# SSD decay factors of one decoder trunk kernel: repeated rows read back from DRAM in place of matmul broadcasts

## Chip, cores and metric

One Trainium2 chip, one core. The metric is the device time of one launch in microseconds (us). The kernel before took 2094.0 us, the median of three runs (2093.61 to 2096.1).

## The reference, cut to what matters

A decoder trunk with 512 tokens, width 1024 and two layers. Each layer is a half SwiGLU feed-forward, a mixer and a second half feed-forward; the mixer of the first layer is a Mamba-2 SSD (state space) mixer, that of the second an S5 mixer. All values are float32. The change touches the SSD mixer alone. It has 32 heads of 64 channels in 8 groups of 4 heads; the group shares B and C (128 states). Per head, with `cs` the running sum of `dt * A` inside a chunk, the reference computes

```python
seg = cs[:, :, None] - cs[:, None]
decay = exp(where(causal, seg, -inf))
cb = einsum('btgn,bsgn->btsg', cc, bc)
dtx = dt[..., None] * xc
y_diag = einsum('btsgk,bsgkp->btgkp', cb[..., None] * decay, dtx)
y_off = einsum('btgn,bgkpn->btgkp', cc, state) * exp(cs)[..., None]
```

and then carries `state` to the next chunk. The kernel uses four chunks of 128 tokens.

## The kernel before

The work runs as stages: feed-forward, SSD, feed-forward, feed-forward, S5, feed-forward. Tokens lie along the free dimension (512 of them), channels along the 128 partitions. A projection (`proj`, L219) multiplies a 1024-wide block with 24 matmuls of 512 columns: every float32 operand is held as a high and a low part, and three products are made for each of 8 blocks. Its weights come on SyncE's queue (SP) in 512 KB loads with four buffers (`wst`); ScalarE casts the high part (L214), VectorE subtracts for the low part (L216), each with three buffers.

**SSD stage (L273 to L545).** First `dt` is projected, and a chain on VectorE and ScalarE (L285 to L314) makes `dt`, the running sums `cs` (L312) and their exponentials; the heads stand in the partitions, 32 heads four times over. Then come 8 groups (loop at L517). Each makes six projections: two convolutions for B and C, two for the channels x (`conv`, L353, `silu`, L368), and two gates (`gate`, L390). The scan of a group is cut in pieces that lie between the projections of the next group, by the list `pend`, from which `pop` (L376) takes one after each projection:

- `head` (L403): products C·B per chunk into `cb`, transposes of x and B, `dtx`, `wx`, and the previous group's `final`
- after the B projection: `states` (L433) and `decay(0)` (L452)
- after the C projection: `outp(0)` (L468) and `decay(1)`
- after the first x projection: `outp(1)`; after the second: nothing; after the first gate: `norm`.

A head pair is one `e` (two heads). `decay(e)` builds, for each of its two heads, a 128x512 tile whose every row is that head's `cs`, by a matmul with a selecting weight (L458, `cshl` holds `cs` as a high and a low part), and adds the causal mask by a second matmul (L459). ScalarE then takes the exponential out of PSUM with the bias -cs of the row's token (L463, one instruction per chunk), and VectorE multiplies by `cb` (L464). `outp(e)` makes exp(cs) for the pair's 128 channels the same way (L473, L475, L477), multiplies it by C·state (L481, L482), makes the diagonal part (L488: 8 float32 matmuls, each recorded as two instructions) and sums, gates and squares (L491 to L495).

After group 4 the first 8 of 16 row blocks of the output projection are done (`out_rows(0, 8)`), after group 7 the rows 8 to 12, between whose eight column blocks the last group's pieces lie, and then the rows 12 to 16.

**What sets the order.** In the SSD stage TensorE's instructions stand in the order in which the program writes them. The instructions of the other engines and queues are ordered by a scheduler with a timing model of its own, unless `tc.keep_in_program_order` puts one behind the instruction that the program wrote before it on the same engine. Every engine and every queue then works strictly in its order. A PSUM tile is 128x512; there are four tagged "mm" (projections) and four tagged "aux". Tiles of a name rotate over their buffers (two where nothing is given).

Of the kernel before, what the change touches and what calls it, by code (L numbers as in the profile page):

```python
# [9 lines left out]
F32 = mybir.dt.float32  # L10
F32R = mybir.dt.float32r
# [19 lines left out]
def trunk_kernel(ctx, tc, x, ffn1_norm, ffn1_w_in, ffn1_w_out, mix_norm, ffn2_norm, ffn2_w_in, ffn2_w_out,  # L31
# [29 lines left out]
    identr = const.tile([128, 128], F32R, name="identr")  # L61
# [6 lines left out]
    def masks():  # L68

        V.tensor_copy(identr, ident)  # L70
# [202 lines left out]
    def ssd(pr, nxt):  # L273
        w_in, w_out = ssd_in_proj[0], ssd_out_proj[0]
        with ExitStack() as es:
            sc = es.enter_context(tc.tile_pool(name="ssdc", bufs=1))
            sp = es.enter_context(tc.tile_pool(name="ssd", bufs=2))

            wd = wpool.tile([128, KD, 128], F32, name="wst", bufs=4)
# [8 lines left out]
            ax = sp.tile([128, T], F32, name="m")  # L288
            V.scalar_tensor_tensor(ax, v, -1.0, v, op0=OP.mult, op1=OP.max)
            ex = sp.tile([128, T], F32, name="m")  # L290
# [5 lines left out]
            rw = sp.tile([128, T], F32, name="m")  # L296
# [3 lines left out]
            dt = sp.tile([128, T], F32, name="m")  # L300
# [15 lines left out]
            for c in range(4):  # L316
# [4 lines left out]
            pack = sp.tile([128, T], F32, name="m")  # L321
# [4 lines left out]
            cshl = sc.tile([128, T], F32R, name="cshl")  # L326
            S.copy(cshl, cs)
            V.tensor_tensor(cshl[32:64], cs[32:64], cshl[32:64].bitcast(F32), op=OP.subtract)
            sel = sc.tile([128, 32], F32R, name="sel")
            V.memset(sel.bitcast(F32), 0.0)  # L330
            V.tensor_copy(sel[0:32], ident[0:32, 0:32])
            V.tensor_copy(sel[32:64], ident[32:64, 32:64])
            mneg = sc.tile([128, 128], F32R, name="mneg")
            mf = sp.tile([128, 128], F32, name="mf", bufs=1)
            G.memset(mf, 0.0)
            G.affine_select(out=mf, in_=mf, compare_op=OP.is_ge, fill=-1e30, base=0, pattern=[[1, 128]],
                            channel_multiplier=-1)
            V.tensor_copy(mneg, mf)
# [14 lines left out]
            def conv(ct):  # L353
# [4 lines left out]
                raw = sp.tile([128, T + 4], F32, name="raw")  # L358
                G.memset(raw[:, 0:4], 0.0)
# [12 lines left out]

            YH, YL = [None] * 16, [None] * 16
# [25 lines left out]
            def scan(g, BT, CT, XS, SZ):  # L399

                st = {}

                def head():  # L403

                    pcb = aux_ps()
                    for c in range(4):
                        s = slice(c * 128, (c + 1) * 128)
                        PE.matmul(pcb[:, s], BT[:, s], CT[:, s], start=True, stop=True)  # L408
# [17 lines left out]
                    for c in range(3):  # L426
                        s = slice(c * 128, (c + 1) * 128)
                        PE.transpose(pbt[:, s], BT[:, s], ident)
# [809 lines left out]
```

## Time and profile before

| | |
|---|---|
| median of three runs | 2094.0 us |
| the profiled execution, its own time | 2095.47 us |
| its span, first to last instruction | 2093.7 us |
| TensorE busy | 2053.9 us, 98% |
| VectorE busy | 1254.8 us, 60% |
| ScalarE busy | 795.8 us, 38% |
| GpSimd busy | 41.0 us, 2% |
| granted TensorE clock, mean | 0.99 of full speed |
| SSD stage, from the `dt` projection to the last output block | about 383 to 830 us of the span |

PE is TensorE's matmuls, PEld its weight loads, DVE VectorE, ACT ScalarE, POOL GpSimd, SP SyncE's queue. A busy time counts from an instruction's start to its recorded end; matmuls overlap, so the step from one start to the next says what one costs. In the rows further down, "aux" and "mm" are the PSUM tiles, "mm" as an operation's output too. "[0.58 <-ACT ecs L477]" behind a row means that the engine stood idle for 0.58 us before it and that the ScalarE instruction of L477 ended that.

### The profile page before, as it was taken

The numbers are of one execution on the slowest core, as the hardware profiler recorded it, in microseconds if no ns is written. First come the engines' busy times: TensorE is split into PE (matmuls) and PEld (weight loads), VectorE is DVE, ScalarE is ACT, GpSimd is POOL, SyncE is SP. The second block draws the span as 40 slices with busy tenths as digits, with TensorE's granted clock in tenths as the row PEclk, the third lists the DMA queues.
The fourth block names the chain that finished last, engine by engine and source line by source line (L and its number), as shares of the span: only waits on it lengthen the run. The fifth ranks groups of instructions, "written<-read, shape, count | busy, mean of one in ns | idle before, by whom it ended". The sixth has DMA issues, their size and how long they took to land.

```text
span 2093.7 us, 27153 instructions
## 1 busy us (share of the span) xinstructions
PE 2053.9 (98%) x10771; PEld 1691.4 (81%) x10771; DVE 1254.8 (60%) x2156; ACT 795.8 (38%) x1149; POOL 41.0 (2%) x114
## 2 busy tenths in 40 slices
PE   8999999999999999999999999999996999999997
PEld 7888888888888887887788888888886888888886
DVE  6889445778875787557764544343458545444444
ACT  5323233566753664333432332222354333222233
POOL 1000000000000000000000000000011000000000
PEclk9999999999999999999999999999997999999999
DMA  6354643322223213535553363333367133333331
GB/s 180 95 159 159 151 108 84 101 71 71 77 70 89 79 41 113 155 110 162 137 146 98 94 200 91 101 94 99 96 189 236 61 91 101 101 91 88 110 87 58
DMA packets 407631, 232.68 MB, mean 111 GB/s; under 512 B 44168, under 2 KB 395568, under 8 KB 407248
## 3 DMA queue, kind: packets, MB, share of 16 engines
q1 hardware_dynamic: 381920, 203.12, 34.2%
q10 hardware_dynamic: 21440, 13.91, 2.3%
q0 software_dynamic: 4144, 13.92, 2.1%
q8 instruction: 84, 1.38, 0.3%
q14 instruction: 43, 0.35, 0.1%
HBM read 206.21 MB, written 24.18 MB: 110 GB/s over the span
## 4 chain that ended last, share of the span: by engine, by line
PE 94%; DVE 3%; ACT 1%; issue 1%; DMA 0%; DVEq 0%; ACTq 0%
PE mm L223 29%; PE mm L225 29%; PE mm L224 29%; PE aux L488 1%; PE aux L481 0%; PE aux L438 0%; DVE z L969 0%; PE aux L149 0%; PE aux L458 0%; PE aux L225 0%; PE aux L223 0%; PE aux L224 0%; PE aux L408 0%; PE aux L827 0%; PE aux L417 0%
## 5 line engine op out<-in xcount | busy, mean ns | idle before, releaser
L214 ACT CAST whi<-wst 128x1024 fp32r<-128x1024 f32 (+2 forms) x357 | 360.9, 1012 | 935.8 <-PE mm L224 652.0
L223 PE MATMUL mm<-hH,whi 128*128 128x512 f32 x1800 | 705.3, 392 | 2.6 <-ACT whi L214 1.6
L225 PE MATMUL mm<-hH,wlo 128*128 128x512 f32 x1800 | 702.0, 390 | 0.5 <-DVE wlo L216 0.5
L224 PE MATMUL mm<-hL,whi 128*128 128x512 f32 x1800 | 702.2, 390 | 0.0
L216 DVE TENSOR_TENSOR wlo<-wst,whi 128x1024 fp32r<-128x1024 f32 (+2 forms) x357 | 418.9, 1174 | 89.8 <-ACT whi L214 85.5
L223 PEld LDWEIGHTS mm<-hH,whi 128*128 128x128 f32 x1800 | 338.2, 188 | 74.1 <-ACT whi L214 2.0
L225 PEld LDWEIGHTS mm<-hH,wlo 128*128 128x128 f32 x1800 | 338.2, 188 | 72.1 <-DVE wlo L216 1.0
L224 PEld LDWEIGHTS mm<-hL,whi 128*128 128x128 f32 x1800 | 338.3, 188 | 69.4 <-issue 0.6
L224 PE MATMUL mm<-al,whi 128*128 128x512 f32 x704 | 275.5, 392 | 0.0
L225 PE MATMUL mm<-ah,wlo 128*128 128x512 f32 x704 | 275.3, 392 | 0.0
L223 PE MATMUL mm<-ah,whi 128*128 128x512 f32 x704 | 274.6, 392 | 0.0
L252 DVE TENSOR_TENSOR up<-mm,rbc 128x512 f32<-128x512 f32 x88 | 60.7, 690 | 220.0 <-PE mm L225 219.8
L264 DVE SCALAR_TENSOR_TENSOR xT<-mm,xT 128x512 f32<-128x512 f32 x96 | 66.1, 690 | 193.3 <-PE mm L225 193.3
L224 PEld LDWEIGHTS mm<-al,whi 128*128 128x128 f32 x704 | 132.1, 188 | 29.0 <-issue 0.6
L223 PEld LDWEIGHTS mm<-ah,whi 128*128 128x128 f32 x704 | 132.1, 188 | 28.7 <-issue 0.6
L225 PEld LDWEIGHTS mm<-ah,wlo 128*128 128x128 f32 x704 | 132.1, 188 | 28.6 <-issue 0.2
L249 DVE TENSOR_TENSOR gt<-mm,rbc 128x512 f32<-128x512 f32 x88 | 60.7, 689 | 147.9 <-PE mm L225 142.9
L255 ACT CAST ah<-up 128x512 fp32r<-128x512 f32 x88 | 54.9, 624 | 67.8 <-DVE up L253 67.7
L364 DVE SCALAR_TENSOR_TENSOR cv<-raw,cols,cv 128x512 f32<-128x512 f32 x96 | 70.9, 745 | 0.7
L253 DVE TENSOR_TENSOR up<-up,gt 128x512 f32<-128x512 f32 x88 | 60.6, 690 | 7.0 <-ACT whi L214 0.5
L257 DVE TENSOR_TENSOR al<-up,ah 128x512 fp32r<-128x512 f32 x88 | 60.0, 684 | 2.4 <-ACT ah L255 1.4
L250 ACT ACTIVATE gt<-gt 128x512 f32<-128x512 f32 x88 | 55.1, 627 | 11.1 <-DVE gt L249 5.3
(341 smaller groups left out, 1727.4 us busy)
## 6 DMA issues: line engine op xcount, KB each, us to landing
wst<-in_ffn_w_in_dram SPq DMA_DIRECT2D x176, 512.0 KB, 3.9
wst<-in_ffn_w_out_dram SPq DMA_DIRECT2D x64, 448.0 KB, 3.7
wst<-in_ssd_in_proj_dram SPq DMA_DIRECT2D x48, 512.0 KB, 4.0
wst<-in_ffn_w_out_dram SPq DMA_DIRECT2D x32, 512.0 KB, 4.0
opP<-d_P SPq DMA_DIRECT2D x16, 512.0 KB, 5.0
wst<-in_s_glu_w_dram POOLq DMA_DIRECT2D x12, 512.0 KB, 5.0
d_t<-p_cs POOLq DMA_DIRECT2D x8, 512.0 KB, 4.3
wst<-in_ssd_out_proj_dram SPq DMA_DIRECT2D x8, 512.0 KB, 4.2
```

The costliest lines, as they stand in the source:

```text
L214: S.copy(hi, st)
L216: V.tensor_tensor(lo, st, hi.bitcast(F32), op=OP.subtract)
L223: PE.matmul(ps, hi[:, k], H[k], start=first and k == 0, stop=False)
L224: PE.matmul(ps, hi[:, k], L[k], start=False, stop=False)
L225: PE.matmul(ps, lo[:, k], H[k], start=False, stop=last and k == n - 1)
L249: V.tensor_tensor(gt, pg, pr.rbc, op=OP.mult)
L250: S.activation(gt, gt, AF.Silu)
L252: V.tensor_tensor(up, pu, pr.rbc, op=OP.mult)
L253: V.tensor_tensor(up, up, gt, op=OP.mult)
L257: V.tensor_tensor(al, up, ah.bitcast(F32), op=OP.subtract)
L264: V.scalar_tensor_tensor(xT[d], po, 0.5, xT[d], op0=OP.mult, op1=OP.add)
L364: V.scalar_tensor_tensor(cv, raw[:, 1 + j:T + 1 + j], col("cw", j * 32 + ct), cv, op0=OP.mult, op1=OP.add)
```

## The change

The cumulative sums `cs` of the 32 heads are written once to a DRAM tile `d_cs` (32 rows of 512, on SP's queue). `rows(e)` reads them back, on GpSimd's queue: one DMA fills a 128x2x512 tile `dec` whose every partition holds the rows of both heads of the pair (512 KB written into SBUF), and two DMAs of 64 partitions each fill the last 384 columns of `ecs` (96 KB each). GpSimd then masks the `dec` tile in place by one `affine_select` of 1024 elements per partition. `exps(e)` is the same eight exponentials, now in place in SBUF, and one for `ecs`, each put behind what the program wrote before it on ScalarE. `decay(e)` is what is left: one product of 1024 elements per partition by `cb`, put behind what the program wrote before it on VectorE. The matmuls of L458, L459 and L475, their operands (`sel`, `selp`, `cshl`, `mneg`, `identr`) and their making go away.

The places: `rows(0)` stands ahead of `head`, `rows(1)` and `exps(0)` behind `head` and the previous `final`, `exps(1)` between `states` and `decay(0)`. The products C·B and the transposes of B leave `head` and stand between the two gates, behind the previous group's `norm` (`chunk_products`). For the last group an empty piece is put in behind `states`, so that the rest comes one output block later. The convolutions' `raw` tiles become two fixed tiles, whose first four columns are cleared once by VectorE rather than 32 times by GpSimd. The `dt` chain's scratch tiles take the new `dec` shape.

The core of the diff (left out: `identr` and its copy, and context lines):

```diff
             sc = es.enter_context(tc.tile_pool(name="ssdc", bufs=1))
             sp = es.enter_context(tc.tile_pool(name="ssd", bufs=2))
 
+            def dec2():
+                m = sp.tile([128, 2, T], F32, name="dec")
+                return m[:, 0], m[:, 1]
+
+
             wd = wpool.tile([128, KD, 128], F32, name="wst", bufs=4)
...
-            ax = sp.tile([128, T], F32, name="m")
+            ax, ex = dec2()
             V.scalar_tensor_tensor(ax, v, -1.0, v, op0=OP.mult, op1=OP.max)
-            ex = sp.tile([128, T], F32, name="m")
             S.activation(ex, ax, AF.Exp, scale=-1.0)
...
-            rw = sp.tile([128, T], F32, name="m")
+            rw, dt = dec2()
             S.activation(rw, ln, AF.Exp, scale=-1.0)
             V.scalar_tensor_tensor(w1, w1, -1.0, ex, op0=OP.add, op1=OP.subtract)
             V.tensor_tensor(w1, w1, rw, op=OP.mult)
-            dt = sp.tile([128, T], F32, name="m")
             V.scalar_tensor_tensor(dt, v, 0.0, ln, op0=OP.max, op1=OP.add)
             V.tensor_tensor(dt, dt, w1, op=OP.subtract)
...
-            pack = sp.tile([128, T], F32, name="m")
+            pack = dec2()[0]
             V.tensor_copy(pack[0:32], dt[0:32])
             V.tensor_scalar(pack[32:64], cs[32:64], -1.0, None, op0=OP.mult)
             V.tensor_tensor(pack[64:128], dt[64:128], ew[64:128], op=OP.mult)
             tok = sc.tile([128, 4, 128], F32, name="tok")
-            cshl = sc.tile([128, T], F32R, name="cshl")
-            S.copy(cshl, cs)
-            V.tensor_tensor(cshl[32:64], cs[32:64], cshl[32:64].bitcast(F32), op=OP.subtract)
-            sel = sc.tile([128, 32], F32R, name="sel")
-            V.memset(sel.bitcast(F32), 0.0)
-            V.tensor_copy(sel[0:32], ident[0:32, 0:32])
-            V.tensor_copy(sel[32:64], ident[32:64, 32:64])
-            mneg = sc.tile([128, 128], F32R, name="mneg")
-            mf = sp.tile([128, 128], F32, name="mf", bufs=1)
-            G.memset(mf, 0.0)
-            G.affine_select(out=mf, in_=mf, compare_op=OP.is_ge, fill=-1e30, base=0, pattern=[[1, 128]],
-                            channel_multiplier=-1)
-            V.tensor_copy(mneg, mf)
+
+            d_cs = dram.tile([32, T], F32, name="d_cs")
+            nc.sync.dma_start(d_cs, cs[0:32])
+
+            def cs_rows(dst, h, parts):
+                n = dst.shape[-1]
+                G.dma_start(dst, bass.AP(tensor=d_cs.tensor, offset=d_cs.offset + h * T + T - n,
+                                         ap=[[0, parts]] + [[T, k] for k in dst.shape[1:-1]] + [[1, n]]))
+
...
-                raw = sp.tile([128, T + 4], F32, name="raw")
-                G.memset(raw[:, 0:4], 0.0)
+                raws.append(raws.pop(0))
+                raw = raws[0]
...
+            raws = [sc.tile([128, T + 4], F32, name=f"raw{i}") for i in range(2)]
+            for raw in raws:
+                V.memset(raw[:, 0:4], 0.0)
             YH, YL = [None] * 16, [None] * 16
...
-            def scan(g, BT, CT, XS, SZ):
+            def chunk_products(BT, CT):
 
                 st = {}
+                pcb = aux_ps()
+                for c in range(4):
+                    s = slice(c * 128, (c + 1) * 128)
+                    PE.matmul(pcb[:, s], BT[:, s], CT[:, s], start=True, stop=True)
+                st["cb"] = sp.tile([128, T], F32, name="cb", bufs=1)
+                S.copy(st["cb"], pcb)
+                pbt = aux_ps()
+                for c in range(3):
+                    s = slice(c * 128, (c + 1) * 128)
+                    PE.transpose(pbt[:, s], BT[:, s], ident)
+                st["bt"] = sp.tile([128, 384], F32, name="btok", bufs=1)
+                S.copy(st["bt"], pbt[:, :384])
+                return st
+
+            def scan(g, st, CT, XS, SZ):
+
 
                 def head():
 
-                    pcb = aux_ps()
-                    for c in range(4):
-                        s = slice(c * 128, (c + 1) * 128)
-                        PE.matmul(pcb[:, s], BT[:, s], CT[:, s], start=True, stop=True)
-                    st["cb"] = sp.tile([128, T], F32, name="cb", bufs=1)
-                    S.copy(st["cb"], pcb)
                     dtx = sp.tile([128, 4, 256], F32, name="dtx", bufs=1)
...
-                    pbt = aux_ps()
-                    for c in range(3):
-                        s = slice(c * 128, (c + 1) * 128)
-                        PE.transpose(pbt[:, s], BT[:, s], ident)
-                    btok = sp.tile([128, 384], F32, name="btok", bufs=1)
-                    S.copy(btok, pbt[:, :384])
-                    st["dtx"], st["wx"], st["bt"] = dtx, wx, btok
+                    st["dtx"], st["wx"] = dtx, wx
...
-                def decay(e):
-
-                    M = []
+                def rows(e):
+
+                    h = 4 * g + 2 * e
+                    m = sp.tile([128, 2, T], F32, name="dec")
+                    cs_rows(m, h, 128)
+                    ecs = sp.tile([128, T], F32, name="ecs")
+                    for hh in range(2):
+                        cs_rows(ecs[hh * 64:hh * 64 + 64, 128:], h + hh, 64)
+                    G.affine_select(out=m.rearrange("p h (c t) -> p (h c) t", c=4),
+                                    in_=m.rearrange("p h (c t) -> p (h c) t", c=4), compare_op=OP.is_ge, fill=-1e30,
+                                    base=0, pattern=[[0, 8], [1, 128]], channel_multiplier=-1)
+                    st["M", e], st["ecs", e] = m, ecs
+
+                def exps(e):
+                    m = st["M", e]
                     for hh in range(2):
                         h = 4 * g + 2 * e + hh
-                        pE = aux_ps()
-                        PE.matmul(pE, sel[:, h:h + 1].to_broadcast([128, 128]), cshl, start=True, stop=False)
-                        PE.matmul(pE, identr, mneg[:, None, :].to_broadcast([128, 4, 128]), start=False, stop=True)
-                        m = sp.tile([128, T], F32, name="m")
                         for c in range(4):
                             s = slice(c * 128, (c + 1) * 128)
-                            S.activation(m[:, s], pE[:, s], AF.Exp, bias=tok[:, c, 32 + h:33 + h])
-                        V.tensor_tensor(m, m, st["cb"], op=OP.mult)
-                        M.append(m)
-                    st["M", e] = M
+                            tc.keep_in_program_order(
+                                S.activation(m[:, hh, s], m[:, hh, s], AF.Exp, bias=tok[:, c, 32 + h:33 + h]))
+                    ecs = st["ecs", e]
+                    tc.keep_in_program_order(S.activation(ecs[:, 128:], ecs[:, 128:], AF.Exp))
+
+                def decay(e):
+
+                    m = st["M", e]
+                    tc.keep_in_program_order(
+                        V.tensor_tensor(m, m, st["cb"][:, None, :].to_broadcast([128, 2, T]), op=OP.mult))
 
                 def outp(e):
                     M = st["M", e]
 
-                    selp = sp.tile([128, 2, 64], F32R, name="selp")
-                    h0 = 4 * g + 2 * e
-                    V.tensor_copy(selp, sel[:, h0:h0 + 2].bitcast(F32)[:, :, None].to_broadcast([128, 2, 64]))
-                    pe_ = mm_ps()
-                    PE.matmul(pe_, selp.rearrange("p a b -> p (a b)"), cshl, start=True, stop=True)
-                    ecs = sp.tile([128, T], F32, name="ecs")
-                    S.activation(ecs[:, 128:], pe_[:, 128:], AF.Exp)
+                    ecs = st["ecs", e]
                     po = aux_ps()
                     for c in range(1, 4):
                         s = slice(c * 128, (c + 1) * 128)
@@ -485,7 +497,7 @@
                         for hh in range(2):
                             s = slice(c * 128, (c + 1) * 128)
                             k0 = (2 * e + hh) * 64
-                            PE.matmul(py[hh * 64:(hh + 1) * 64, s], st["dtx"][:, c, k0:k0 + 64], M[hh][:, s], start=True,
+                            PE.matmul(py[hh * 64:(hh + 1) * 64, s], st["dtx"][:, c, k0:k0 + 64], M[:, hh, s], start=True,
                                       stop=True)
...
-                return both(head, *fin), [both(states, lambda: decay(0)), both(lambda: outp(0), lambda: decay(1)),
+                rows(0)
+                return both(head, *fin, lambda: rows(1), lambda: exps(0)), [
+                    both(states, lambda: exps(1), lambda: decay(0)), both(lambda: outp(0), lambda: decay(1)),
                                           lambda: outp(1), lambda: None, norm], final
...
@@ -527,9 +541,10 @@
                     SZ.append(gate(2 * g + e, f"sz{e}"))
                     if e == 0:
                         pop()
+                        st = chunk_products(BT, CT)
                 while pend:
                     pop()
-                head, pend, last = scan(g, BT, CT, XS, SZ)
+                head, pend, last = scan(g, st, CT, XS, SZ)
                 if g:
                     head()
                 else:
@@ -537,6 +552,7 @@
                 fin = [last]
                 if g == 4:
                     out_rows(0, 8)
+            pend[1:1] = [lambda: None]
```

## Rows read from the trace of the kernel before

**Rows 1.** The page, parts 1 and 4: busy times, chain that ended last

```profile
PE 2053.9 (98%) x10771; PEld 1691.4 (81%) x10771; DVE 1254.8 (60%) x2156; ACT 795.8 (38%) x1149; POOL 41.0 (2%) x114
...
PE 94%; DVE 3%; ACT 1%; issue 1%; DMA 0%; DVEq 0%; ACTq 0%
```

**Rows 2.** Stretches: length, then busy us of PE, PEld, DVE, ACT, POOL

```profile
511.00:555.00 44.00, 44.00 (x294) 36.58 (x293) 35.38 (x66) 28.84 (x46) 0.41 (x4) 1.00 0.27 73
527.49:536.01 8.52, 8.52 (x52) 7.04 (x51) 7.52 (x12) 6.27 (x15) 0.10 (x1) 1.00 0.23 63
774.00:830.00 56.00, 54.53 (x336) 44.11 (x335) 45.42 (x83) 29.07 (x56) 0.00 (x0) 1.00 0.29 85
```

**Rows 3.** Waits of TensorE's matmuls, 372 to 830 us: total, times, longest

```profile
PE aux L149 <- ACT sq L495: 1.0, 1, 1.0
PE aux L158 <- DVE nw_y L140: 0.9, 1, 0.9
PE aux L481 <- DVE st L448: 0.5, 1, 0.5
```

**Rows 4.** Groups of instructions by line: count, busy us, mean ns, idle before

```profile
L458 PE MATMUL aux<-cshl,sel 128*128 128x512 f32 x32 | 15.0, 468 | 0.0
L475 PE MATMUL mm<-cshl,selp 128*128 128x512 f32 x16 | 6.3, 393 | 0.0
L464 DVE TENSOR_TENSOR m<-m,cb 128x512 f32<-128x512 f32 x32 | 22.0, 688 | 2.4 <-ACT m L463 2.2
```

**Rows 5.** Timeline of TensorE around one `decay(0)`: start us, us

```profile
520.70 0.58 PE L458 MATMUL aux<-cshl,sel 128*128 128x512 f32 x1
521.12 0.40 PE L459 MATMUL aux<-mneg,identr 128*128 128x512 f32 x1
...
521.82 0.39 PE L223 MATMUL mm<-hH,whi 128*128 128x512 f32 x1
```

**Rows 6.** TensorE's timeline around `outp(0)`, `decay(1)` and the next `outp(1)`

```profile
527.29 0.39 PE L475 MATMUL mm<-cshl,selp 128*128 128x512 f32 x1
528.28 1.09 PE L488 MATMUL aux<-m,dtx 128*64 128x128 f32 x16
529.31 0.51 PE L458 MATMUL aux<-cshl,sel 128*128 128x512 f32 x1
...
530.34 0.39 PE L223 MATMUL mm<-hH,whi 128*128 128x512 f32 x1
...
536.80 1.09 PE L488 MATMUL aux<-m,dtx 128*64 128x128 f32 x16
```

**Rows 7.** Timeline of VectorE in the same stretch

```profile
530.30 0.55 DVE L482 TENSOR_TENSOR ecs<-ecs,aux 128x384 f32<-128x384 f32 x1 [0.58 <-ACT ecs L477]
...
538.78 1.23 DVE L216 TENSOR_TENSOR wlo<-wst,whi 128x1024 fp32r<-128x1024 f32 x1 [1.95 <-ACT whi L214]
```

**Rows 8.** GpSimd's mask (ns min/median/max), and a GpSimd copy beside VectorE (timeline)

```profile
L336 POOL TENSOR_SCALAR_AFFINE_SELECT mf<-mf x1: 287/287/287, 383.5 to 383.5; 128x128 f32<-128x128 f32 x1
...
359.86 2.56 POOL L282 COPY wst<-wst 128x256 f32<-128x256 f32 x3 [140.56 <-DVE xT L264]
...
361.28 0.88 DVE L176 TENSOR_TENSOR acc<-acc,sq 128x512 f32<-128x512 f32 x1
...
365.99 0.68 DVE L176 TENSOR_TENSOR acc<-acc,sq 128x512 f32<-128x512 f32 x1
```

**Rows 9.** The page, part 6: 512 KB loads on SP's and GpSimd's queues

```profile
wst<-in_ssd_in_proj_dram SPq DMA_DIRECT2D x48, 512.0 KB, 4.0
wst<-in_s_glu_w_dram POOLq DMA_DIRECT2D x12, 512.0 KB, 5.0
```

**Rows 10.** VectorE's `selp` and `cs` (first and last start); first B projection

```profile
L473 DVE CAST selp<-sel x16: 164/217/218, 384.3 to 755.9; 128x128 fp32r<-128x128 f32 x16
...
L312 DVE TENSOR_TENSOR_SCAN y<-rst,y x1: 1205/1205/1205, 406.7 to 406.7; 128x512 f32<-128x512 f32 x1
...
389.32 0.39 PE L223 MATMUL mm<-hH,whi 128*128 128x512 f32 x1
```

More of the change, by code (lines that the diff above doesn't have):

```diff
@@ L60, in trunk_kernel @@
     make_identity(nc, ident)
-    identr = const.tile([128, 128], F32R, name="identr")
     ones = const.tile([128, 128], F32, name="ones")
@@ L68, in masks @@
     def masks():
-        V.tensor_copy(identr, ident)
         V.tensor_reduce(kmask, ident.rearrange("p (k q) -> p k q", q=8), axis=AX.X, op=OP.add)
```

## Prediction, made before the changed kernel was run

> **What bounds the kernel now.** I read the page first: TensorE is busy for 98% of the span, and 94% of the chain that ended last is TensorE's [rows 1]. That is an average over six stages, so I then read the SSD stage by stretches and by TensorE's waits. In a steady group TensorE is busy for all of the stretch, VectorE for 35 of 44 us, ScalarE for 29, GpSimd for 0.4 [rows 2]. In the whole stage its matmuls wait three times, 2.4 us together: 1.0 us in the first group's scan, 0.9 and 0.5 us in the last's [rows 3]. So here a matmul that goes away is worth its step from start to start, not its recorded 393 or 468 ns [rows 4], as long as nothing that was hidden behind TensorE comes out.
>
> **What goes from TensorE.** 16 head pairs (8 groups, two each) lose four broadcast and mask matmuls in `decay` and one in `outp`. In a first `decay` the step from the first L458 to the next projection is 521.82 - 520.70 = 1.12 us [rows 5], in a second 530.34 - 529.31 = 1.03 us [rows 6]. The first L458 takes a step of 0.42 us, the three behind it 521.82 - 521.12 = 0.70, so 0.233 each [rows 5]: the first stands behind float32 matmuls. I expect that extra to pass to the projection matmul that follows in its place, so four plain steps remain, 4 x 0.233 = 0.93 us; if it vanished, 1.12 and 1.03 would. L475 is a plain step too: it stands behind a projection and is counted 16 times [rows 4]. That is 16 x (0.93 + 0.23) = 18.6 us, at most 16 x 0.23 + 8 x (1.12 + 1.03) = 20.9 us. All of it lies on the path that sets the end.
>
> `chunk_products` moves 7 matmul calls, which cost TensorE the same where they go. They stand right behind the previous group's `norm`, also float32, so as a rule no change between kinds of matmul is added. In groups 0 and 5 other pieces stand there or none (group 4's have been taken by `out_rows(0, 8)`): at most one extra step of 0.42 - 0.23 = 0.19 us [rows 5], so 0.2 us.
>
> **The waits.** The first group's 1.0 us is `norm` waiting for ScalarE's square; that chain loses the ecs exponential, for which VectorE idles 0.58 us even in a steady group [rows 7]. I take 1.0 us as gone, bounds 0 and 1.0. The 0.5 us at L481 has a whole output block more in the new order: gone, bounds 0 and 0.5. The 0.9 us wait of `final` for `norm` keeps the same distance and stays, bounds from a gain of 0.9 to a loss of as much, since `final` now has one output block behind it instead of two.
>
> **What is added, and its cover.** DMAs on GpSimd's queue: three per pair, 48 in all, 16 x (512 + 2 x 96) KB = 11 MB. A 512 KB load on that queue lands after 5.0 us [rows 9]. A pair's `dec` buffer comes free at the end of the same pair's `outp` one group earlier, and its first use is the exponentials behind `head`, some 24 us later for `rows(0)` (L488 at 528.3, the group's end at 555 [rows 2, 6]), the next B projection later still for `rows(1)`. Load and mask have to fit in that. Cost nothing; were the cover gone, 5 to 8 us a pair. The DMA engines are at 0.27 in this stage [rows 2]; SP's weight loads, 4.0 us each [rows 9], have four buffers ahead of them.
>
> The mask: 128 columns took 0.287 us [rows 8], so 1024 take at most 8 x 0.287 = 2.3 us; 16 of them are 37 us of an engine that has 0.4 us to do per group. On GpSimd's queue each stands behind its DMAs, and the next pair's DMAs behind it; both waits end long before the use. The 32 clears of `raw` leave this queue.
>
> SP's queue: the one write of `cs`, behind which weight loads queue. It is ready at 406.7 + 1.2 = 407.9 us [rows 10]. The scheduler orders by readiness: `selp` (L473) is written behind `cs` in the program, and yet the first of its 16 ran at 384.3, 22 us ahead of `cs` [rows 10]. So I expect the write to stand where `cs` is ready, a wait of a few us at most, with loads ahead. Cost nothing.
>
> ScalarE: the same eight exponentials per pair and one for ecs, but all nine together, `exps(1)` pinned behind B's `silu`. Behind them on ScalarE wait the next weight casts, which are three buffers ahead of TensorE. VectorE: 16 `selp` casts of 0.217 us [rows 10] go, and two products of 0.688 us [rows 4] become one of twice the width.
>
> Here is the tight place. `decay(1)` is now pinned behind `outp(0)`'s last VectorE instruction, and both heads' product must be whole before `outp(1)`'s first L488. L488 to L488 is 536.80 - 528.28 = 8.52 us [rows 6] and becomes 8.52 - 1.16 = 7.36 us. VectorE was busy 7.52 of the 8.52 us in that place [rows 2]; less the cast and 0.15 us for one product instead of two, some 7.15 us. It just fits, and the convolution's and the weights' subtractions among these 7.15 us may also come behind the product. So zero, bounds 0 and 1.5 us a group (the second product's length again and the exponentials' tail).
>
> While GpSimd copied at 359.9 to 362.4, L176 on VectorE took 0.88 us, and 0.68 us a little later [rows 8]: 0.2 us of slowing for an instruction beside it. A mask of 2.3 us may so touch three instructions, 0.6 us, mostly outside the tight place: its data land about 5 us behind L488, and VectorE later idles 1.95 us before one instruction [rows 7]. The Trainium skill ("SBUF — State Buffer", section "Who interferes with whom") says more: a VectorE instruction with two SBUF inputs and a GpSimd instruction that reads SBUF exclude each other, the second blocked until the first ends. By that rule a product could be held for the whole mask; the row shows a fraction of it, so the sum goes by the row.
>
> **Sum.** 18.6 - 0.2 + 1.0 + 0.5 = 19.9 us; for the small losses around the last `final` and the exponentials' start I take back 0.9 us: 19 us. The profiled execution took 2095.5 us by its own time (span 2093.7), so 2076.5; it lies 1.5 us above the median of 2094.0. Against the median: 2075.
>
> **Rivals.**
> 1. The product comes late. For: the count above leaves 0.2 us. Against: the exponentials are done earlier than before, and VectorE has no other wait there. Price 0.3 to 1.5 us in each of 7 groups, 2 to 10 us: 2077 to 2085, middle 2080. 18%.
> 2. A mask holds VectorE in the tight place for its whole length, 2.3 us less the spare 0.2, in each of 7 groups: 15 us, so 2090. Against: the mask's data come after the product's turn, and the row shows 0.2 us [rows 8]. 5%. The lock of the Trainium skill ("SBUF — State Buffer", as above) would act this way.
> 3. The rows don't come early, so the change doesn't do what it says: if 128 reads of one row of DRAM are slow, or the queue's order puts one pair's load behind another's wait. ScalarE would wait in front of the weights' casts. 24 us of cover must be used up first; beyond it, at about 1 us a pair, 16 us is given back: 2091, about the same as before. 4%.
> 4. Slower: the `cs` write stands in SP's queue where the program writes it, ahead of the first B weights. They would start at 407.9, land 4.0 us later [rows 9] and need the subtraction, 1.23 us [rows 7], and a cast of about as much: 414.3, where the B projection now starts at 389.3 [rows 10]. 25 us lost against 19 gained: 2100. It decides from a hold of 19 us on. Against: the `selp` row. 4%.
>
> **How the numbers follow.** The forecast, 2073 to 2077, has 69%. The low end takes in the upper bounds of the removed steps and waits: 20.9 + 2.4 = 23.3 us, 2071. Upward, rivals 2 to 4 hold 13% and are left out, except for the near part of a late product: 2086. A measurement of this kernel can tell about 0.2%, 4 us: faster means below 2090. Forecast, rival 1 and a part of 2 are faster: 0.89; the rest of 2 and 3 are the same: 0.06; rival 4 and worse holds: 0.05.
>
> **What would show it.** Right: no L458, L459, L475; L481 directly behind a projection; groups 2.3 us shorter, where the steady stretch is 44 us now [rows 2]; TensorE's waits near 1 us in the stage; the `dec` loads and masks over well before their exponentials. A late product would show as L488 waiting for VectorE's product line, a lock as VectorE instructions of 2 to 3 us beside GpSimd's mask, late rows as ScalarE waiting for GpSimd, a held queue as a TensorE gap near 390 to 414 us. A gain under 10 us or over 24 us would make the forecast wrong.

## The result, and the profile after

The changed kernel takes 2083.7 us (median of four runs, 2081.72 to 2084.14), the kernel before, beside it, 2094.0: a ratio of 0.9947 (95% interval 0.993 to 0.9964; intervals stand in brackets below). That is 10.3 us faster, where 19 were forecast; the time lies inside the range and in the place of rival 1, a late product. The profiled execution took 2084.14 us, its span is 2082.4 us (before 2093.7).

The page's busy times, its shares of the chain that ended last, and its row for the new loads (answering to [rows 1, 9]):

```profile
PE 2036.1 (98%) x10691; PEld 1675.3 (80%) x10691; DVE 1255.1 (60%) x2120; ACT 793.8 (38%) x1144; POOL 83.4 (4%) x144
...
PE 91%; DVE 4%; ACT 3%; issue 2%; POOL 0%; DVEq 0%; ACTq 0%; POOLq 0%
...
dec<-d_cs POOLq DMA_DIRECT2D x16, 512.0 KB, 4.2
```

TensorE has 17.8 us less to do, but its share of the chain fell from 94 to 91%, and ScalarE's rose from 1 to 3%: work of others has come onto the path. The waits of TensorE's matmuls in the SSD stage, 372 to 830 us, show which (answering to [rows 3]; L500 is the former L488, L493 the former L481):

```profile
PE aux L500 <- DVE dec L484: 6.3, 7, 1.7
PE aux L156 <- DVE nw_y L138: 1.6, 3, 0.9
PE aux L493 <- DVE st L452: 0.7, 1, 0.7
PE aux L427 <- ACT xs L367: 0.5, 1, 0.5
PE mm L221 <- ACT yh L519: 0.3, 1, 0.3
PE mm L222 <- DVE yl L521: 0.2, 1, 0.2
```

9.6 us in place of 2.4. The diagonal part waits for the product seven times: once in the first group (1.7 us), five times in steady groups (about 0.8 each), once in the last (0.7). The wait of the last group is that of the first pair: its product stands right behind the carried state's last sum on VectorE (779.19 and 779.53 us).

18.6 us taken off, less 7.2 us of new waits, is 11.4 us, and the span is 11.3 us shorter; but that agreement is in part luck. The stage, from the sum of squares ahead of the first group (`ones,sq`, at 386.56 us before) to the last matmul of the output projection (832.19), took 445.6 us before and takes 435.8 now: 9.8 us less. The other 1.5 us lie outside it, where the change touches nothing, and where profiled executions differ by as much among themselves (from 1560 to 1620 us the granted clock was 0.74 in the one before, 0.80 in this one).

One steady group as a stretch, from one `norm` to the next (length, then busy us of PE, PEld, DVE, ACT, POOL; answering to [rows 2]):

```profile
502.50:544.69 42.19, 41.38 (x283) 34.40 (x282) 35.54 (x60) 26.67 (x45) 5.90 (x8) 1.00 0.37 110
```

The same step in the kernel before:

```profile
505.26:548.92 43.66, 43.66 (x292) 36.31 (x291) 35.09 (x65) 28.84 (x47) 0.41 (x4) 1.00 0.27 74
```

It should have lost five plain steps twice, 2 x (0.93 + 0.23) = 2.32, and so take 41.34; it takes 42.19, and TensorE is idle for 0.81 of the 0.85 us that are missing. Where they come from stands in the timelines of TensorE, ScalarE and VectorE in that group (start us, us; answering to [rows 6, 7]):

```profile
530.92 0.83 PE L493 MATMUL aux<-CT,st 128*128 128x128 f32 x6
532.56 1.09 PE L500 MATMUL aux<-dec,dtx 128*64 128x128 f32 x16 [0.81 <-DVE dec L484]
...
525.32 1.28 ACT L367 ACT_TABLE_LOAD   x1
526.62 0.72 ACT L367 ACTIVATE BT<-cv,cols 128x512 f32<-128x512 f32 x1
527.36 1.28 ACT L476 ACT_TABLE_LOAD   x1
528.65 2.45 ACT L476 ACTIVATE dec<-dec,tok 128x128 f32<-128x128 f32 x8
...
529.11 0.68 DVE L505 TENSOR_TENSOR y<-y,sz 128x512 f32<-128x512 f32 x1
531.20 1.31 DVE L484 TENSOR_TENSOR dec<-dec,cb 128x1024 f32<-128x1024 f32 x1 [1.40 <-issue]
```

VectorE is done with the first pair's output at 529.79 and stands idle for 1.40 us. The product starts only after the last of the second pair's exponentials (528.65 + 2.45 = 531.10), and so it does in the first and in every steady group: 0.1 us behind that exponential's end. Those were put behind B's `silu` (526.62), which needs its own function table, and the exponentials need theirs back: two loads of 1.28 us around a silu of 0.72. A product begun at 529.7 with its 1.22 us would have been whole at 530.9, before the diagonal part's normal turn, 0.76 us behind L493, at 531.68.

What the prediction had costed at nothing, in the rows of the tile `dec` (ns min/median/max, first to last start):

```profile
L464 POOL TENSOR_SCALAR_AFFINE_SELECT dec<-dec x16: 1087/1089/1707, 417.4 to 752.5; 128x1024 f32<-128x1024 f32 x16
L484 DVE TENSOR_TENSOR dec<-dec,cb x16: 1218/1220/1311, 442.3 to 784.3; 128x1024 f32<-128x1024 f32 x16
```

The mask takes 1.09 to 1.71 us, under the bound of 2.3, and the loads land 4.2 us after issue. GpSimd's timeline has one mask at 530.34 and the next at 537.70, and the exponentials that read these tiles are in a later group: no row of the stage has TensorE waiting for rows, mask or weights.

### The profile page after: what moved, and what is told of

Same layout as the page of the kernel before. It is cut to its first block, busy times and chain, and to the rows that moved or that the text cites. A ratio compares the mean times of both kernels' runs of the same rounds, so it can differ in the third digit from the quotient of the medians.

```text
span 2082.4 us, 27026 instructions
## 1 busy us (share of the span) xinstructions
PE 2036.1 (98%) x10691; PEld 1675.3 (80%) x10691; DVE 1255.1 (60%) x2120; ACT 793.8 (38%) x1144; POOL 83.4 (4%) x144
## 3 DMA queue, kind: packets, MB, share of 16 engines
q8 instruction: 84, 1.38, 0.3%
## 4 chain that ended last, share of the span: by engine, by line
PE 91%; DVE 4%; ACT 3%; issue 2%; POOL 0%; DVEq 0%; ACTq 0%; POOLq 0%
PE mm L221 29%; PE mm L222 28%; PE mm L223 28%; ACT dec L476 1%; DVE dec L484 1%; ACT L476 1%; PE aux L500 1%; DVE wlo L214 0%; PE aux L1003 0%; ACT L367 0%; DVE z L985 0%; ACT whi L212 0%; PE aux L222 0%; PE aux L223 0%; PE aux L221 0%
## 5 line engine op out<-in xcount | busy, mean ns | idle before, releaser
L361 DVE SCALAR_TENSOR_TENSOR cv<-raw,cols,cv 128x512 f32<-128x512 f32 x96 | 76.6, 804 | 14.0 <-ACT cv L359 13.2
```

The lines of the kernel that those rows point to most:

```text
L361: V.scalar_tensor_tensor(cv, raw[:, 1 + j:T + 1 + j], col("cw", j * 32 + ct), cv, op0=OP.mult, op1=OP.add)
```

## The experiments

The expectations speak of three theories. **A**: the second pair's exponentials come late, by their place on ScalarE. **B**: the product comes late by its place in VectorE's queue. **C**: a mask on GpSimd holds VectorE. All kernels were timed in rounds against the kernel before, which took 2095.28 us beside the first four, 2095.99 beside the next four and 2095.59 beside the last four; the times are medians. The changed kernel was timed beside 2094.0, so 1 to 2 us between kernels of different rounds can be a difference of the rounds. The stage's length by the traces, one execution each, leaves out what happens elsewhere: 435.8 us in the changed kernel, 449.3, 444.9 and 442.9 in runs 1 to 3, 435.2 in run 4, 431.7 in run 5, 433.7 in run 6, 429.5 in run 7, 436.9 in run 8, 429.6 in run 9, 434.1, 429.5 and 435.1 in runs 10, 11 and 12. What lies behind the stage, the same in all kernels, took from 1259.4 to 1262.6 us. Line numbers are those of each kernel.

**1. The exponentials of both pairs together, ahead of the B convolution's silu.**

```diff
-return both(head, *fin, lambda: rows(1), lambda: exps(0)), [
-    both(states, lambda: exps(1), lambda: decay(0)), ...
+return both(head, *fin, lambda: rows(1), lambda: exps(0), lambda: exps(1)), [
+    both(states, lambda: decay(0)), ...
```

> The second pair's exponentials stand directly behind the first pair's, behind head, in place of behind the B silu. Theory A (they are late on ScalarE, behind the B silu and two table loads, and the product and L500 wait for them): the seven waits of L500 for the product, 6.3 us together, go; time 2083.7 less 6 to 8, so 2076 to 2078. Theory B (the pin puts the product too late among VectorE's own work): waits stay, 2083 to 2085. Theory C (the mask on GpSimd holds VectorE in that place): waits stay or shrink by a third, 2081 to 2084.

Measured 2096.93 us, 1.0007 [0.9998, 1.0016]: all of the gain was gone, and the waits of L500 rose to 14.8 us. By its name the wait is the same; the timelines of ScalarE, VectorE and TensorE say otherwise (the last row is TensorE's stretch behind the wait; the 0.50 in it is the granted clock):

```profile
527.46 0.71 ACT L359 ACTIVATE cv<-raw,cols 128x512 f32<-128x512 f32 x1
...
528.20 0.75 DVE L361 SCALAR_TENSOR_TENSOR cv<-raw,cols,cv 128x512 f32<-128x512 f32 x1 [2.40 <-ACT cv L359]
...
538.78 1.98 PE L500 MATMUL aux<-dec,dtx 128*64 128x128 f32 x16 [2.48 <-DVE dec L484]
...
538.78:540.76 1.98, 1.98 (x17) 1.65 (x17) 1.98 (x4) 1.33 (x2) 0.00 (x0) 0.50 0.03 9
```

The sixteen exponentials now end at 527.1, 8 us ahead of the L493 of 535.47; in the changed kernel they end 0.2 us behind it. But the B convolution's first tap, which ScalarE makes, stands behind them, and VectorE idles 2.40 us in front of its second tap. Later it has no gap left, and the product comes at 537.42. So ScalarE's block can be late for two users, the product and the convolution. That points to a place with one pair's exponentials on each side of the tap. Theory A had the user right and the cure wrong. The stage's waits are 8.0 us longer. Behind four of the five waits of about 2.5 us TensorE's clock fell to its lower level (granted 0.50, 1.2 GHz), and such a group takes 45.43 us where 41.35 and the wait of 2.48 give 43.83: 1.6 us each. Waits and clock make 14.4 us; 13.2 were lost.

**2. The product not pinned on VectorE.**

```diff
-tc.keep_in_program_order(
-    V.tensor_tensor(m, m, st["cb"][:, None, :].to_broadcast([128, 2, T]), op=OP.mult))
+V.tensor_tensor(m, m, st["cb"][:, None, :].to_broadcast([128, 2, T]), op=OP.mult)
```

> The product by cb is no longer pinned on VectorE; all else as in the changed kernel. Theory A: the product still needs the exponentials, so it starts no earlier; 2083 to 2085. Theory B: the scheduler moves it forward and the waits of L500 go, 2076 to 2078. Theory C: no change.

Measured 2093.03 us, 0.9987 [0.9978, 0.9996]. The waits for the product went from 6.3 to 7.9 us (longest 1.7), those for `nw_y` from 1.6 to 3.8, for `st` from 0.7 to 2.0. Neither theory's number: the pin is worth 9 us. The stage's waits are 5.4 us longer. Behind two of them, of 1.73 us in the first group and 1.98 us in the last, the granted clock fell to 0.50: six or seven projection matmuls each time have steps of 0.43 us instead of 0.23, and the ones beside them are longer too, some 3 us together. That makes 8.5 of the 9.3 us.

**3. The exponentials not pinned on ScalarE** (`tc.keep_in_program_order` taken away from the nine activations of `exps`).

> The exponentials are no longer pinned on ScalarE; all else as in the changed kernel. Theory A: the time follows where the second pair's exponentials end. If they come later than now, as the scheduler's own order has them behind the first x silu, both pairs' products are late, L500 waits some us in each group, and the time is above 2094, slower than before the change. Theory B and C: 2083 to 2085, as VectorE and GpSimd have the same work.

Measured 2093.68 us, 0.9995 [0.9986, 1.0004]. The waits for the product all but vanish (1.0 us), and others take their place:

```profile
PE aux L427 <- ACT xs L367: 3.3, 5, 1.7
PE aux L405 <- ACT CT L367: 3.2, 1, 3.2
PE aux L156 <- ACT cb L407: 2.5, 1, 2.5
```

The scheduler's own order has the exponentials early, not late as was expected: in a steady group they end 25 us ahead of the product (513.6 and 538.56 us). There C, the x tiles and the copy of the products C·B wait for ScalarE. The product stands behind the first pair's output as in the changed kernel, so the vanished waits speak for theory A. The pins are worth 10 us, of which the stage's longer waits (13.5 us in place of 9.6) show 3.9 and the lower clock behind the wait of 3.2 us some 1.5; the rest, 4.6, stays open.

**4. No mask.** The bias is changed and a scale of 1e-6 given, so that the exponentials stay small and are as many.

```diff
-G.affine_select(out=m..., compare_op=OP.is_ge, fill=-1e30, ...)
-    S.activation(m[:, hh, s], m[:, hh, s], AF.Exp, bias=tok[:, c, 32 + h:33 + h]))
+    S.activation(m[:, hh, s], m[:, hh, s], AF.Exp, bias=tok[:, c, h:h + 1], scale=1e-6))
```

> GpSimd's mask is left out, and the exponentials take dt as bias and scale their input down, so that they stay finite (the decay factors are not the reference's); as many instructions on every other engine. Theory A: the exponentials still end when they do, behind the B silu, so 2083 to 2084, at most 1 us less. Theory C: VectorE is free of the mask, the waits of L500 go, 2076 to 2078.

Measured 2081.71 us, 0.9939 [0.9926, 0.9951]; the waits for the product still total 5.8 us in seven places, where 6.3 were to be explained: theory C doesn't explain the loss. The time is 2 us lower, more than theory A allowed, but the intervals overlap; by the traces the stage is 0.6 us shorter, and a steady step takes 42.06 us instead of 42.19.

**5. The second pair's exponentials between the B convolution's first tap and its silu**, in groups 1, 2, 3, 5 and 6.

```diff
-    both(states, lambda: exps(1), lambda: decay(0)), ...
+    both(states, lambda: g in (0, 4, 7) and exps(1), lambda: decay(0)), ...
...
-BT = silu(conv(16 + g), 16 + g, "BT")
+cvb = conv(16 + g)
+while g > 1 and early:
+    early.pop(0)()
+BT = silu(cvb, 16 + g, "BT")
```

> In groups 1, 2, 3, 5 and 6 the second pair's exponentials stand between the B convolution's first tap on ScalarE and the B silu, so that they end some 5 us earlier, need no table loads of their own, and do not stand in front of that tap as in the run with all of them behind head. Theory A (in the changed kernel L500 waits for the product because the second pair's exponentials end late on ScalarE; in the first experiment it waited because ScalarE's block of 16 held up the convolution's tap and so VectorE): the waits of these five groups, 0.80 to 0.88 us each, go, those of the first and last group stay: 2083.7 - 4.2, so 2079 to 2080. Theory B (VectorE's own work makes the product late whenever): they stay at 0.8 us or more, 2083 to 2086.

Measured 2080.13 us, 0.9924 [0.9911, 0.9938]: 3.6 us faster than the changed kernel. The waits, one steady group from `norm` to `norm`, and the timelines of TensorE and ScalarE in it:

```profile
PE aux L500 <- DVE dec L484: 2.5, 2, 1.7
...
499.76:541.11 41.35, 41.35 (x282) 34.40 (x282) 36.21 (x60) 23.91 (x43) 6.43 (x8) 1.00 0.38 111
...
528.18 0.83 PE L493 MATMUL aux<-CT,st 128*128 128x128 f32 x6
528.94 1.09 PE L500 MATMUL aux<-dec,dtx 128*64 128x128 f32 x16
...
518.97 2.43 ACT L476 ACTIVATE dec<-dec,tok 128x128 f32<-128x128 f32 x8
```

All five waits of the steady groups are gone, TensorE is busy for the whole stretch, and the stretch is 41.35 us: the 41.34 that the removed matmuls give. The waits of the stage add up to 5.7 us, 3.9 less than in the changed kernel. ScalarE is busy for 2.8 us less in the group, mostly two table loads fewer (2 x 1.28). The product's place on VectorE is the same, between the first pair's output and the same tap, so this confirms theory A for the steady groups. Place and table loads were changed together; what each is worth was not tried. What is left is the first group's wait and the last's.

**6. The second product written ahead of the first pair's output.**

```diff
-both(lambda: outp(0), lambda: decay(1)),
+both(lambda: decay(1), lambda: outp(0)),
```

> decay(1)'s product is written, and so pinned, ahead of outp(0)'s VectorE work in place of behind it; the exponentials stay late. Theory A: the product can start no earlier than the exponentials end, and now holds up outp(0)'s sums meanwhile: no gain, 2084 to 2090. Theory B: the product runs some 2 us earlier and the waits go, 2076 to 2078.

Measured 2081.38 us, 0.9927 [0.9915, 0.994], between the two theories' ranges. The waits of L500 stay (6.5 us in seven places; in the same group 0.81 us as before). But this is no test of theory B, since only the pin moved. VectorE and ScalarE in that group:

```profile
527.41 0.68 DVE L505 TENSOR_TENSOR y<-y,sz 128x512 f32<-128x512 f32 x1
528.02 0.73 DVE L361 SCALAR_TENSOR_TENSOR cv<-raw,cols,cv 128x512 f32<-128x512 f32 x1
529.49 1.30 DVE L484 TENSOR_TENSOR dec<-dec,cb 128x1024 f32<-128x1024 f32 x1 [0.74 <-issue]
...
526.95 2.45 ACT L476 ACTIVATE dec<-dec,tok 128x128 f32<-128x128 f32 x8
```

The first pair's output isn't pinned, and the scheduler kept it ahead: the product now has one more tap in front of it, and still starts 0.1 us behind the last exponential (529.40). Only in the scans of groups 4 and 7, beside the output projection, does it go ahead of the output. The 2.3 us come from smaller waits there (`nw_y` 1.6 to 0.9, `st` 0.7 to 0.4; those for `xs` and `yh`, 0.5 and 0.3, gone): 1.6 us in all, as L500's grew by 0.2. By the traces the stage is 2.1 us shorter; the step from group 4's `norm` to the next takes 42.6 us instead of 44.2.

**7. Both edits, 5 and 6.**

> Both edits: exponentials between tap and silu, product ahead of outp(0)'s VectorE work. Theory A: the waits of the five groups go, 2079 to 2080, as without the second edit. If both theories hold in part (ScalarE's end and VectorE's order each cost something), this is the fastest of the three, 2077 to 2079.

Measured 2077.21 us, 0.9909 [0.9895, 0.9922]; in the steady groups the product stands behind the first pair's output here too. The waits of the stage fall to 4.0 us (L500 2.5 in two places, `nw_y` 0.9, `st` 0.4, `yl` 0.2).

**8. The products C·B and the transposes back in `head`** (the call of `chunk_products` moved from between the gates into `head`).

> The products C·B and the transposes of B go back to the head; all else as in the changed kernel. TensorE has the same work; its seven calls leave the place behind norm. Theory A: the second pair's exponentials and so the waits stay as they are, 2083 to 2085. If that part of the change was worth something by itself, because ScalarE's copies of them now stand in front of the first pair's exponentials, the time is 2086 or more.

Measured 2085.03 us, 0.9945 [0.9932, 0.9957], so 1.3 us more than the changed kernel, with overlapping intervals. Two waits of `final` for ScalarE's copy of `cb` appear (2.6 us), and the stage's waits grow from 9.6 to 10.9 us, by the same 1.3. By the trace that part of the change is worth about 1 us; the times can't tell it from nothing.

**9. Edit 7, and the first group's second pair between the C convolution's tap and its silu.**

```diff
-CT = silu(conv(24 + g), 24 + g, "CT")
+cvc = conv(24 + g)
+while early:
+    early.pop(0)()
+CT = silu(cvc, 24 + g, "CT")
```

> As the last version (exponentials between tap and silu, product first), and the first group's second pair too, between the C convolution's tap and the C silu. Theory A: L500's wait in the first group, 1.7 us, goes as well: 2077.2 - 1.7, so 2075 to 2076; only the last group's 0.7 us stays. Theory B: no change, 2077 to 2078.

Measured 2076.61 us, 0.991 [0.9896, 0.9923], no faster than run 7 within the intervals, and its stage is as long (429.6 and 429.5 us). The first group's wait stayed, against the expectation. Its timelines (TensorE, ScalarE, VectorE, GpSimd):

```profile
452.12 1.09 PE L500 MATMUL aux<-dec,dtx 128*64 128x128 f32 x16 [1.84 <-DVE dec L484]
...
441.60 2.43 ACT L476 ACTIVATE dec<-dec,tok 128x128 f32<-128x128 f32 x8
...
441.89 1.53 DVE L361 SCALAR_TENSOR_TENSOR cv<-raw,cols,cv 128x512 f32<-128x512 f32 x2
...
449.26 1.58 DVE L361 SCALAR_TENSOR_TENSOR cv<-raw,cols,cv 128x512 f32<-128x512 f32 x1
450.77 1.21 DVE L484 TENSOR_TENSOR dec<-dec,cb 128x1024 f32<-128x1024 f32 x1
...
448.15 2.14 POOL L464 TENSOR_SCALAR_AFFINE_SELECT dec<-dec 128x1024 f32<-128x1024 f32 x1 [3.37 <-DMA dec<-d_cs]
```

The exponentials are done at 444.0, and still the product starts at 450.77: VectorE has no gap at all from 441.89 on. Here it is VectorE that is full, with a second convolution's taps, and the last of them takes 1.58 us instead of 0.74 beside a mask. In the changed kernel, too, VectorE stood idle for just 0.56 us ahead of this product. So in the first group two causes ended nearly together, and with one removed the other held the wait. Both removed at once was not tried.

**10. Edit 7 with every mask done twice.**

```diff
+G.affine_select(out=m..., in_=m..., compare_op=OP.is_ge, fill=-1e30, ...)
```

> The version with exponentials between tap and silu and the product first, with GpSimd's mask made twice (the second changes nothing). Theory A: VectorE has room again, so the 16 masks of 1.1 to 1.7 us more on GpSimd cost under 1 us: 2077 to 2078. Theory C (what a mask holds up on VectorE lies on the path): 16 times up to 0.8 us more on VectorE, L500 waits again, 2079 to 2085.

Measured 2081.27 us, 0.9931 [0.9919, 0.9944], 4.1 us more than edit 7. The steady step is 41.39 us, as without it; the first group pays:

```profile
454.20 1.38 PE L503 MATMUL aux<-dec,dtx 128*64 128x128 f32 x16 [3.30 <-DVE dec L487]
...
451.38 2.77 DVE L487 TENSOR_TENSOR dec<-dec,cb 128x1024 f32<-128x1024 f32 x1
```

There the product stood beside a mask and took 2.77 us instead of 1.22. This is what rival 2 described, in the one group where VectorE has no slack. The time is in theory C's range, but by this group alone. The stage's waits grew by 2.6 us, and behind the wait of 3.30 us the granted clock was 0.61 for 3 us (454.2 to 457.2): the diagonal part took 1.38 us instead of 1.09, and five projection matmuls behind it have steps of 0.43 instead of 0.23. That is about 1.6 us, and both together are the 4.1.

**11. Edit 7 without the mask** (as in 4).

> The same version with the mask left out (and dt as the exponentials' bias, their input scaled down, so the decay factors are not the reference's). Theory A: within 1 us of it, 2076 to 2078, and the VectorE instructions of 1.5 us beside the masks are 0.75 us again. Theory C: 2 us or more less, 2075 or under.

Measured 2078.16 us, 0.9916 [0.9903, 0.993], 1 us more than with the mask and within the intervals; the first wait stays (2.4 us in two places), by the late exponentials there. So with the exponentials placed well, one mask per pair costs nothing that the times or the stage's length (429.5 us in both) show. What it does to VectorE is seen in the taps' row (count, busy us, mean ns), first of run 7, then of run 11:

```profile
L361 DVE SCALAR_TENSOR_TENSOR cv<-raw,cols,cv 128x512 f32<-128x512 f32 x96 | 73.3, 769 | 4.5 <-ACT cv L359 3.6
```

```profile
L361 DVE SCALAR_TENSOR_TENSOR cv<-raw,cols,cv 128x512 f32<-128x512 f32 x96 | 70.9, 745 | 9.0 <-ACT cv L359 8.2
```

745 ns is the mean of the kernel before; the masks add 2.4 us to the taps in the whole stage.

**12. Edit 7 without the empty piece for the last group** (`pend[1:1] = [lambda: None]` taken out).

> The same version without the empty piece in the last group. The last group's outp(0) then comes one output block (2.8 us) earlier, before its product is ready: L500 and L493 wait there some 2 us in place of 1.1 us, and final has two blocks behind it again: 2078 to 2080. If the empty piece was worth nothing: 2077.

Measured 2083.25 us, 0.9939 [0.9926, 0.9953]: the empty piece is worth 6 us, more than was expected. TensorE's timeline in the last group, and its stretches there:

```profile
771.74 0.49 PE L493 MATMUL aux<-CT,st 128*128 128x128 f32 x2 [2.03 <-DVE st L452]
773.17 0.49 PE L493 MATMUL aux<-CT,st 128*128 128x128 f32 x2 [0.94 <-DVE st L452]
774.39 1.98 PE L500 MATMUL aux<-dec,dtx 128*64 128x128 f32 x16 [0.74 <-DVE dec L484]
...
774.39:776.37 1.98, 1.98 (x17) 1.65 (x17) 0.32 (x1) 0.00 (x0) 0.00 (x0) 0.50 0.06 17
776.50:778.00 1.50, 1.50 (x4) 1.21 (x5) 1.43 (x3) 0.00 (x0) 0.00 (x0) 0.50 0.00 0
```

The carried state is late by 2.03 and 0.94 us, where edit 7 waits 0.4 in all. Behind these waits the granted clock falls to 0.50, that is 1.2 GHz: the sixteen matmuls take 1.98 us instead of 1.09, and nine projection matmuls behind them have steps of 0.43 instead of 0.23. The waits cost 2.6 us more, the clock 0.9 + 9 x 0.2 = 2.7: 5.3 of the 6 us.

## Why the prediction was right in part

**TensorE's term was right.** 16 x (0.93 + 0.23) = 18.6 us, with the extra of the first broadcast passed on to the projection: a steady step without waits is 41.35 us against 43.66 (runs 5, 7 and 9: 41.35 to 41.39), at most 2.31 less, where 2.32 was worked out.

**The covers were right.** The loads, masks, weight loads, casts and the write of `cs` cost TensorE nothing that a row shows. Rivals 3 and 4 fell. The mask took at most 1.71 us in the changed kernel, but 2.3 us is no bound: in run 7 single masks took up to 2.82, and no wait came of it.

**The waits were half right.** The 1.0 us of `norm` went. The 0.5 us of L481 did not: its successor L493 waits 0.7 us in the last group, though an output block more lies ahead of it. The 0.9 us of `final` stayed at 0.9, with two waits of about 0.3 beside it.

**The step that failed** is the argument against rival 1: "the exponentials are done earlier than before, and VectorE has no other wait there". I counted VectorE's work between two diagonal parts, found it to fit just so, and took ScalarE's nine exponentials as early because they stand ahead in the program. I didn't lay them out on ScalarE: behind B's silu, with a table load before and behind it, they end 1.3 us after VectorE is free. So the term "zero, bounds 0 and 1.5 us a group" was 0.8 us in five groups and 1.7 in the first; with the last group's 0.7 that is 6.3 us in all. The time lies in the range because the range takes in rival 1's price. Rival 1's mechanism, VectorE's own work, wasn't the cause, so that its price fits is luck: in the steady groups the product waited for ScalarE. Run 5 shows it by taking the wait away with the product's place unchanged, and run 3, where the exponentials end 25 us ahead, does too. VectorE's fullness is real too: it decides in the first group (run 9), in the last, where another product than rival 1's is late, and everywhere once its taps are held up (run 1).

**Rival 2's mechanism exists**, larger than the row that I went by: beside a mask a tap takes 1.58 us instead of 0.74, not 0.2 us more. A VectorE instruction with two SBUF inputs and a GpSimd instruction that reads SBUF exclude each other, says the Trainium skill ("SBUF — State Buffer", section "Who interferes with whom"). The 0.84 us more in run 9 agree with that better than with my 0.2, and the mask's growth from 1.09 to 2.14 us agrees too: two VectorE instructions with two inputs run in its first 1.2 us (448.00 to 449.34), and about 1 us behind them it ends. Run 10's row doesn't follow so simply: the product began 0.56 us ahead of the mask (451.38 and 451.94), and yet the mask took its 1.11 us and the product 1.55 more; spans on GpSimd are rough. In the steady groups the mask lay off the path, and there it cost 0.1 us (run 4) or nothing (run 11).

**The empty piece** had 0.5 us in my sum. Run 12 puts it at 6, in the kernel of edit 7; in the changed kernel itself it was not taken out. The waits that it covers are longer than the one in the kernel before, and they take the clock with them. Against the kernel before, edit 7 gains 18.8 us with it and 12.3 without.

The removed steps less run 7's waits are 18.6 - 4.0 + 2.4 = 17.0 us, where 18.8 were measured. Its stage is 16.1 us shorter than before, so the other 2.7 lie outside the stage. Against run 5 its stage is 2.2 us shorter, by the smaller waits of run 6. Open are the 0.9 us between 17.0 and 16.1 and the 4.6 us of run 3's loss that neither waits nor clock show (its stage is 7.1 us longer than the changed kernel's, so 1.7 of them lie in the stage).

## What to carry to other kernels

When a matmul is replaced by work of other engines, write out the in-order queue of each engine on the new path, table loads included, and not only of the engine that comes last: here 3.6 us hung on whether eight exponentials stood before or behind one silu. Moving a block earlier isn't free either; it delays whatever stands behind it, and the right place was a gap between two users. And read the queue again after an edit: in run 6 the product was written earlier and yet ran behind the same instructions, since these weren't pinned. Where two engines are both tight, a wait that stays after a cure may have a second cause of the same length.

## What the runs showed of the hardware that was not expected

- A wait of TensorE can be followed by its lower clock level (granted 0.50, 1.2 GHz), and the length of that wait alone doesn't say whether. In run 1 the clock fell behind four waits of 2.45 to 2.56 us and not behind a fifth of 2.47; in run 2 it fell behind one of 1.73, while behind one of 1.73 in the changed kernel and of 1.84 in run 9 it stayed. Rows of run 1, then of run 2:

```profile
584.20 1.09 PE L500 MATMUL aux<-dec,dtx 128*64 128x128 f32 x16 [2.47 <-DVE dec L484]
...
452.38 1.09 PE L499 MATMUL aux<-dec,dtx 128*64 128x128 f32 x16 [1.73 <-DVE dec L483]
...
454.22 0.63 PE L223 MATMUL mm<-hH,wlo 128*128 128x512 f32 x1
454.65 0.63 PE L221 MATMUL mm<-hH,whi 128*128 128x512 f32 x1
```

  So a wait can have a second price, 1.5 to 2.7 us each time here, up to about the size of the first.
- A VectorE product beside a GpSimd mask took 2.77 us instead of 1.22 (run 10), a tap 1.58 instead of 0.74 (run 9), and a mask up to 2.82 instead of 1.09 (run 7); without the mask the taps' mean is the 745 ns of the kernel before (run 11).
- A load that writes the same two rows of DRAM into each of 128 partitions was not slow here: 512 KB landed in 4.2 us, against 3.9 us for the weights beside it.
